# Score products of 128 rows with a copied low part of k, and a second gate projected ahead of the first branch product

## The chip, the cores and the metric

The kernel runs on one core of a Trainium2 chip. The metric is the device time of one execution in microseconds (us); the time of a kernel is the median over several executions. The core has five engines with a queue of instructions each: TensorE (PE in the profile; its weight loads are shown apart as PEld), VectorE (DVE), ScalarE (ACT), GpSimd (POOL) and SyncE (SP), which here issues nearly all of the transfers. On-chip memory is SBUF with 128 partitions; matmul results go to PSUM.

## The reference

One decoder layer on 1024 tokens of width 1024, in float32:

- `u = x * (1 + scale) + shift`, with shift, scale and gates from a small product of the conditioning vector.
- One projection of `u` gives q, k, v of two mixers and two gates of width 1024, `ga` and `gb`.
- Mixer a: 16 query heads of 64 over 2 key heads, causal window of 128, with a sink in the softmax denominator. Mixer b: 24 heads of 64 in three dilations (1, 4, 16), 8 heads each, whose outputs are weighted by the softmax of their log-sum-exps.
- Scores are `s = (q . k) / 8` in blocks of 128 queries against at most 256 keys.
- `merged = sigmoid(ga) * (oa @ w_branch_a) + sigmoid(gb) * (ob @ w_branch_b)`, then `merged @ w_o`, a residual with layer norm, a SwiGLU feed-forward of width 2816, and a second residual with layer norm.

## The kernel before, in words

**Exactness.** Matmuls take a rounded float32 format. An operand is therefore split into a high part (a rounding copy on ScalarE) and a low part (what is left, by a subtraction on VectorE), and a product is three matmuls: high x high, high x low, low x high (`mac`, lines 136 to 139, whose lines 137 to 139 lead the profile).

**Stage one, attention.** Twenty units follow each other: twelve of mixer b (four head pairs times three dilations, in the text "dilated units") and eight of mixer a ("window units"). A unit has two heads of 64 that lie in the lower and the upper 64 partitions. A generator `stream` yields the projections: of a dilated unit k, v and q, of a window unit q, and for the first of them also v and, last, k, which all eight share. One step of it is six matmuls; `pump` interleaves these steps with the four groups of scores of the unit before, the exponentials, the transposes of the probabilities (line 544) and the products with v (line 567). Work after a projection is put off by some steps (`soon`), so that TensorE doesn't wait for it. All of this is an order written by hand: each engine works its own queue in the order of the program.

The split of k is `k_stacks` (443 to 464). After rotary (GpSimd writes the result `r`, line 420), for each head ScalarE writes the high part `kh` twice, into the head's own 64 partitions (line 448) and into the other 64 (line 449), and VectorE writes the low part `kl` into the own half (line 454); only for the k that the window units share it writes the other half as well (line 456). The split of q (`q_stacks`) puts q's high part into the own half and its low part into the other. So one matmul of 128 rows against `kh` gives (high q + low q) x high k. A group of scores (`scores`, line 485) is for two blocks of queries and two heads: four such matmuls of 128 rows (line 495), then four of 64 rows with high q x low k (line 501), where the heads use different halves of the rows. A block is 256 keys wide, or 128 where there is no previous block.

**Weights.** `Weights` brings the weight pieces (256 KB each) in three raw buffers by SP (line 55), and splits them into four pairs of buffers `w_hi`, `w_lo` (lines 78 and 79). A piece is sent for as soon as a raw buffer is free; `step` splits the next one, at two points of a projection.

**Stage two, branch products.** For each of three branch halves (the two halves of `w_branch_a`, then `w_branch_b`) and eight column blocks `dc`, four split parts of the attention output, `o_hl` (line 117 high, 118 low), are multiplied with one weight piece and merged. Gates are projected in between by `make_gate` (48 matmuls, 16 groups of three): number 8 + dc for `ga`, 16 + dc for `gb`. Three gates (dc 3, 4, 5) are already projected in stage one, kept in device memory in `ga_d`, and only loaded. The list `order` fixes the sequence: gate 8 comes first, then products 0 to 7, then gate 9, product 8, gate 10, product 9 and so on. Ahead of gate 8 the parts of the first half are split (`o_parts`). Between gate groups and products `next(ada)` takes one of about forty small steps of a conditioning sum.

Of the kernel before, what the change touches and what calls it, by code (L numbers as in the profile page):

```python
# [10 lines left out]
F32 = mybir.dt.float32  # L11
F32R = mybir.dt.float32r
I32 = mybir.dt.int32
AF = mybir.ActivationFunctionType
OP = mybir.AluOpType
# [3 lines left out]
P = 128  # L19
T = 1024  # L20
# [78 lines left out]
def decoder_layer(ctx: ExitStack, tc: tile.TileContext, I, out, dbg=None):  # L99
    nc = tc.nc  # L100
# [54 lines left out]
    steps = [(b, dc) for b in range(3) for dc in range(KC)]  # L155
    gate_of = {8 + dc: 46 + dc for dc in range(KC)}
    gate_of.update({16 + dc: 54 + dc for dc in range(KC)})
    branch_w = [I["w_branch_a"][0], I["w_branch_a"][1], I["w_branch_b"]]
    made_early = [8 + dc for dc in (early_gate_dc, *tail_gates)]
    order = []  # L160
    for i in range(len(steps)):
        g = 8 if i == 0 else i + 1
        if g in gate_of and i != 7:
            order.append(("g", g))
        order.append(("w", i))
    for kind, i in order:
        if kind == "g" and i not in made_early:
            add_chunk(I["w_in"][gate_of[i]], 2, 4)
        elif kind == "w":
            b, dc = steps[i]  # L170
            add_chunk(branch_w[b][dc], 1, 4)
# [40 lines left out]
    ga_d = dram.tile([KC, P, T], F32, name="ga_d")  # L212
# [143 lines left out]
    att = ph1.enter_context(tc.tile_pool(name="att", bufs=2, side="right", reuse_waits="tile"))  # L356
# [69 lines left out]
    LO, HI = slice(0, 64), slice(64, 128)  # L426
# [13 lines left out]

        return rotary(e, r, then)

    def k_stacks(e, r, both, box):

        def stack(res, h):
            own, other = ((LO, HI), (HI, LO))[h]
            kh = att.tile([P, T], F32R, name="kh", bufs=4)
            nc.scalar.activation(kh[own], res[own], AF.Copy)
            nc.scalar.activation(kh[other], res[own], AF.Copy)
            box.setdefault("kh", []).append(kh)  # L450
            los = box.setdefault("kl", [])
            if both or not los:
                los.append(att.tile([P, T], F32R, name="kl", bufs=2))
            nc.vector.tensor_tensor(los[-1][own], res[own], kh[own], op=OP.subtract)  # L454
            if both:
                nc.vector.tensor_tensor(los[-1][other], res[own], kh[own], op=OP.subtract)
            elif h:
                los.append(los[0])

        def then(res):  # L460
            for h in range(2):
                soon(2 + h + (2 if e < EARLY else 0), lambda h=h: stack(res, h))

        return rotary(e, r, then)
# [20 lines left out]
    def scores(un, qr):  # L485

        box, prev, st = un["box"], un["prev"], un["st"]
        probs = att.tile([P, 2, 2, 2, P], F32, name="probs", bufs=2)
        un["probs", qr] = probs
        khs, kls = (box["kh"], box["kl"]) if "kv" not in un else ([kv_a["kh"][un["kv"]]] * 2, [kv_a["kl"][un["kv"]]] * 2)  # L490
        pss = [ps_s.tile([P, 2, 2, P], F32, name="s") for _ in range(2)]
        blocks = [(i, 2 * qr + i, 0 if prev(2 * qr + i) else 1) for i in range(2)]
        for i, b, lo in blocks:
            for h in range(2):
                nc.tensor.matmul(pss[h][:, i, lo:], box["q"][h][:, b * P:(b + 1) * P],  # L495
                                 khs[h][:, (b - 1 + lo) * P:(b + 1) * P], start=i == 0, stop=False,
                                 skip_group_check=True)

        for i, b, lo in blocks:
            for h, own in enumerate((LO, HI)):  # L500
                nc.tensor.matmul(pss[h][:, i, lo:], box["q"][h][own, b * P:(b + 1) * P],  # L501
                                 kls[h][own, (b - 1 + lo) * P:(b + 1) * P], start=False, stop=i == 1,
                                 skip_group_check=True)
        mx = att.tile([P, 2, 2], F32, name="mx", bufs=3)
        for h in range(2):
            for i, b, lo in blocks:
                nc.vector.tensor_tensor_reduce(  # L507
                    out=probs[:, h, i, lo:], in0=pss[h][:, i, lo:], in1=un["mask"][:, lo:], scale=QS, scalar=NEG,
                    op0=OP.add, op1=OP.max, accum_out=mx[:, h, i:i + 1])
            sl = slice(2 * qr, 2 * qr + 2)  # L510
            if "kv" in un:
                nc.vector.tensor_scalar(st[:, 0, h, sl], mx[:, h], un["sink"](h), -1.0, op0=OP.max, op1=OP.mult)  # L512
            else:
                nc.vector.tensor_scalar(st[:, 0, h, sl], mx[:, h], -1.0, None, op0=OP.mult)
# [150 lines left out]
    kv_a, units = {}, []  # L665
# [8 lines left out]
    def sigmoid_half(dst, ps):  # L674
        nc.scalar.activation(dst, ps, AF.Tanh, scale=0.5)
        nc.vector.tensor_scalar(dst, dst, 0.5, 0.5, op0=OP.mult, op1=OP.add)

    def stream():
        for un in units:
            if "b" in un:  # L680
                p, g = un["b"]
                base, r = (p * 3 + g) * 3, B_DIL[g]
                yield from k_stacks(base, r, False, un["box"])
                yield from values(base + 1, r, un["box"])
                yield from q_stacks(base + 2, r, un["box"])
            else:
                yield from q_stacks(36 + un["a"] + 2 * (un["a"] > 0), 1, un["box"])
                if un["a"] == 0:
                    yield from values(37, 1, kv_a)
                    yield from k_stacks(38, 1, True, kv_a)  # L690
        for dc in tail_gates:
            g = att.tile([P, T], F32, name="r", bufs=1)
            yield from project(46 + dc, lambda t, ps: sigmoid_half(g[:, t * TH:(t + 1) * TH], ps))
            nc.sync.dma_start(ga_d[dc], g)
# [49 lines left out]
    for s in range(len(subs) + 2):  # L744
        n, i = divmod(s, 4)
# [103 lines left out]
    ada = ada_steps()  # L849
    gts = {}  # L850

    def make_gate(i, *steps):
        g = mix.tile([P, T], F32, name="gt", bufs=2)
        gts[i] = g
        if i in made_early:
            nc.sync.dma_start(g, ga_d[i - 8])
            return
        ps = [ps_2.tile([P, TH], F32, name="p2") for _ in range(2)]
        for n, t in enumerate(gemm_u(ps, ws.take(2), *steps)):
            if n % 4 == 2:  # L860
                next(ada, None)
            if t is not None:
                sigmoid_half(g[:, t * TH:(t + 1) * TH], ps[t])

    def merge(b, dc, t, ps, g):
        m = mrg(dc, t)
# [18 lines left out]
                    nc.sync.dma_start(dbg["mg"][dc * P:(dc + 1) * P, t * TH:(t + 1) * TH], mrg(dc, t))  # L885

    for kind, i in order:
        if kind == "g":
            if i in (8, 9, 17):
                ws.prepare(4)  # L890
                parts = o_parts({8: 0, 9: 1, 17: 2}[i])
                make_gate(i, ())
            else:
                make_gate(i)
            if i == 23:
                mg = wide("m", bigu)
                split_merged(range(0, 3))
            continue
# [515 lines left out]
```

## Time and profile before

| | us |
|---|---|
| median of three runs | 1885.06 |
| lowest and highest run | 1883.31 and 1887.6 |
| the profiled execution's own time | 1886.68 |
| its span, first to last instruction | 1884.6 |
| TensorE busy in it | 1827.5 (97%) |
| VectorE, ScalarE, GpSimd busy | 1154.8, 784.0, 600.0 |

The mean granted clock of TensorE over the span is 0.992 of full speed. Busy time of an engine counts overlapping instructions once. A row of the profile has the line of the kernel, the engine, the operation, what is written <- what is read, shapes and a count; behind the bar stand total busy time and the mean in ns of one, and the engine's idle time in front with what ended it. A row of the order of time begins with the start in us from the span's start and the duration; a square bracket holds the idle time of the engine before it and what it waited for. `q` behind an engine is its queue of issues.

### The profile page before, as it was taken

Reading aid. Unit: us, or ns where it says so; the run is one execution under the profiler, and the core shown is the slowest. Engines: PE = TensorE matmul, PEld = TensorE weight load, DVE = VectorE, ACT = ScalarE, POOL = GpSimd, SP = SyncE. Lnnn points to the kernel's source line nnn. Section 1 sums busy time; section 2 is a strip of 40 time slices with the busy share of each in tenths; the row PEclk is TensorE's granted clock in tenths of the full one; section 3 lists DMA queues with packets and bytes.
Section 4 is the critical chain, followed back from the end, with each engine's and each line's share of the span. In section 5 each row is a group of like instructions: output and inputs, shape, how many; then the busy total and the mean of one; then the engine's idle time right before and its main releaser. Section 6 shows DMA issues by size and latency. Waiting matters only on the chain.

```text
span 1884.6 us, 24305 instructions
## 1 busy us (share of the span) xinstructions
PE 1827.5 (97%) x8924; PEld 1475.4 (78%) x8924; DVE 1154.8 (61%) x2136; ACT 784.0 (42%) x1664; POOL 600.0 (32%) x389
## 2 busy tenths in 40 slices
PE   6899999999999999989999999999999999999998
PEld 3678887877878767768888878878888888888886
DVE  5865567667667887643645365575565444674567
ACT  3544454544454667743112132653433333421122
POOL 2422323223223312100312242455664333531223
PEclk9999999999999999999999999999999999999999
DMA  8211112112111132144543223122222222442222
GB/s 280 91 34 35 35 36 79 40 39 76 42 57 63 41 95 76 57 168 155 208 137 137 79 72 134 57 90 101 85 78 85 89 79 89 151 134 71 97 84 89
DMA packets 72408, 171.85 MB, mean 91 GB/s; under 512 B 13089, under 2 KB 14177, under 8 KB 72290
## 3 DMA queue, kind: packets, MB, share of 16 engines
q1 hardware_dynamic: 71954, 169.26, 26.3%
q8 instruction: 70, 1.15, 0.3%
q0 software_dynamic: 336, 1.06, 0.2%
q14 instruction: 48, 0.39, 0.1%
HBM read 146.33 MB, written 23.95 MB: 90 GB/s over the span
## 4 chain that ended last, share of the span: by engine, by line
PE 81%; DVE 9%; ACT 4%; issue 3%; POOL 2%; DMA 1%; DVEq 0%; SPq 0%; POOLq 0%; ACTq 0%
PE pf L1108 22%; PE pj L137 7%; PE pj L139 7%; PE pj L138 6%; PE p L138 5%; PE p L139 5%; PE p L137 5%; PE pf L138 5%; PE pf L139 5%; PE pf L137 5%; PE pt L544 2%; PE po L567 2%; PE s L495 1%; PE s L501 1%; DVE probs L507 1%
## 5 line engine op out<-in xcount | busy, mean ns | idle before, releaser
L137 PE MATMUL pj<-u,w_hi 128*128 128x512 f32 x720 | 301.1, 418 | 0.0
L139 PE MATMUL pj<-u,w_lo 128*128 128x512 f32 x720 | 283.7, 394 | 0.0
L138 PE MATMUL pj<-u,w_hi 128*128 128x512 f32 x720 | 282.5, 392 | 0.0
L419 POOL TENSOR_TENSOR rb<-rb,sin_t 128x512 f32<-128x512 f32 x64 | 86.7, 1355 | 502.5 <-DVE rb L417 438.0
L118 DVE TENSOR_TENSOR w_lo<-r,w_hi 128x512 fp32r<-128x512 f32 x110 | 116.2, 1059 | 138.8 <-ACT w_hi L117 137.8
L79 DVE TENSOR_TENSOR w_lo<-w_raw,w_hi 128x512 fp32r<-128x512 f32 x148 | 131.2, 890 | 85.2 <-ACT w_hi L78 83.0
L522 ACT ACTIVATE probs<-probs,st 128x128 f32<-128x128 f32 (+1 forms) x320 | 146.0, 460 | 59.3 <-DVE st L512 30.1
L137 PEld LDWEIGHTS pj<-u,w_hi 128*128 128x128 f32 x720 | 136.2, 189 | 33.4 <-issue 4.7
L139 PEld LDWEIGHTS pj<-u,w_lo 128*128 128x128 f32 x720 | 135.8, 189 | 30.4
L138 PEld LDWEIGHTS pj<-u,w_hi 128*128 128x128 f32 x720 | 136.5, 190 | 22.4
L138 PE MATMUL pf<-wd,h 128*128 128x512 f32 x352 | 137.1, 389 | 0.0
L139 PE MATMUL pf<-wd,h 128*128 128x512 f32 x352 | 137.1, 389 | 0.0
L137 PE MATMUL pf<-wd,h 128*128 128x512 f32 x352 | 137.1, 389 | 0.0
L62 POOL TENSOR_TENSOR w_raw<-w_raw,gate 128x512 f32<-128x512 f32 x60 | 85.5, 1439 | 143.9 <-DMA w_raw<-in_w_down 120.6
L1327 DVE SCALAR_TENSOR_TENSOR zt<-zt,pf 128x512 f32<-128x512 f32 x112 | 75.3, 685 | 79.7 <-PE pf L139 79.7
L420 POOL TENSOR_TENSOR r<-ra,rb 128x512 f32<-128x512 f32 x63 | 114.5, 1817 | 6.1 <-DVE kl L454 1.3
L78 ACT ACTIVATE w_hi<-w_raw 128x512 fp32r<-128x512 f32 x148 | 90.8, 624 | 33.9 <-PE p L138 16.8
L546 ACT ACTIVATE ptsb<-pt 128x512 f32<-128x512 f32 (+1 forms) x128 | 63.5, 547 | 93.4 <-PE pt L544 93.0
L137 PE MATMUL p<-o_hl,w_hi 128*128 128x512 f32 x192 | 76.1, 396 | 6.8 <-ACT o_hl L117 6.8
L137 PE MATMUL p<-u,w_hi 128*128 128x512 f32 x208 | 82.2, 395 | 0.0
L139 PE MATMUL p<-u,w_lo 128*128 128x512 f32 x208 | 81.1, 390 | 0.0
L138 PE MATMUL p<-u,w_hi 128*128 128x512 f32 x208 | 81.0, 389 | 0.0
(305 smaller groups left out, 4266.8 us busy)
## 6 DMA issues: line engine op xcount, KB each, us to landing
w_raw<-in_w_in SPq DMA_DIRECT2D x116, 256.0 KB
r<-in_w_gate_up SPq DMA_DIRECT2D x47, 512.0 KB
a_raw<-in_w_ada SPq DMA_DIRECT2D x32, 512.0 KB
w_raw<-in_w_down SPq DMA_DIRECT2D x44, 256.0 KB
h_raw<-h_d SPq DMA_DIRECT2D x22, 512.0 KB
h_d<-g SPq DMA_DIRECT2D x40, 256.0 KB
wa<-in_w_ada_m SPq DMA_DIRECT2D x16, 512.0 KB
wb<-wt_d SPq DMA_DIRECT2D x24, 256.0 KB
```

What stands on the lines that cost most here:

```text
L62: self.nc.gpsimd.tensor_tensor(self.raws[i], self.raws[i], scale(), op=OP.mult)
L78: self.nc.scalar.activation(hi, raw, AF.Copy)
L79: self.nc.vector.tensor_tensor(lo, raw, hi, op=OP.subtract)
L118: nc.vector.tensor_tensor(lo, src, hi, op=OP.subtract)
L137: nc.tensor.matmul(ps, w[0], m[0], start=first, stop=False)
L138: nc.tensor.matmul(ps, w[0], m[1], start=False, stop=False)
L139: nc.tensor.matmul(ps, w[1], m[0], start=False, stop=last)
L419: eng.tensor_tensor(b, b, sin_t[:, s], op=OP.mult)
L420: eng.tensor_tensor(residue_half(res, r, t), by_residue(a, r), by_residue(b, r), op=OP.add)
L522: nc.scalar.activation(pr, pr, AF.Exp, bias=st[:, 0, h, b:b + 1], accum_out=st[:, 1, h, b:b + 1])
L1108: nc.tensor.matmul(ps, w[:, c], m[:, k], start=first and k == 0 and n == 0, stop=k == 3 and n == 2, skip_group_check=True)
L1327: nc.vector.scalar_tensor_tensor(z, z, ALPHA if gi == 0 else 1.0, pd, op0=OP.mult, op1=OP.add)
```

## The change

1. `k_stacks` makes both parts full height for every k: ScalarE writes `kh` into the own half only, VectorE `kl` into the own half only, and each is copied into the other half by a transfer that SP issues (SBUF to SBUF, 64 partitions x 4 KB). `kl` has four buffers in place of two.
2. `scores` uses `kl` with all 128 rows. For each block and head the product with `kh` is followed at once by that with `kl`; low q x low k is now part of the sum.
3. Gate 10 (dc 2 of `ga`) is projected right after gate 8, ahead of the first branch product, and written to `ga_d`. In its old place it is loaded, as the three early gates are. While it is projected no step of the conditioning sum is taken.

```diff
+    bridge = 10
     order = []
     for i in range(len(steps)):
         g = 8 if i == 0 else i + 1
         if g in gate_of and i != 7:
             order.append(("g", g))
+        if i == 0:
+            order.append(("b", bridge))
         order.append(("w", i))
     for kind, i in order:
-        if kind == "g" and i not in made_early:
+        if kind == "b" or (kind == "g" and i not in (*made_early, bridge)):
             add_chunk(I["w_in"][gate_of[i]], 2, 4)
...
-    def k_stacks(e, r, both, box):
+    def k_stacks(e, r, box):
...
             kh = att.tile([P, T], F32R, name="kh", bufs=4)
+            kl = att.tile([P, T], F32R, name="kl", bufs=4)
             nc.scalar.activation(kh[own], res[own], AF.Copy)
-            nc.scalar.activation(kh[other], res[own], AF.Copy)
+            nc.sync.dma_start(kh[other].bitcast(F32), kh[own].bitcast(F32))
+            nc.vector.tensor_tensor(kl[own], res[own], kh[own], op=OP.subtract)
+            nc.sync.dma_start(kl[other].bitcast(F32), kl[own].bitcast(F32))
             box.setdefault("kh", []).append(kh)
...
+            box.setdefault("kl", []).append(kl)
...
             for h in range(2):
-                nc.tensor.matmul(pss[h][:, i, lo:], box["q"][h][:, b * P:(b + 1) * P],
-                                 khs[h][:, (b - 1 + lo) * P:(b + 1) * P], start=i == 0, stop=False,
-                                 skip_group_check=True)
-
-        for i, b, lo in blocks:
-            for h, own in enumerate((LO, HI)):
-                nc.tensor.matmul(pss[h][:, i, lo:], box["q"][h][own, b * P:(b + 1) * P],
-                                 kls[h][own, (b - 1 + lo) * P:(b + 1) * P], start=False, stop=i == 1,
-                                 skip_group_check=True)
+                for n, ks in enumerate((khs, kls)):
+                    nc.tensor.matmul(pss[h][:, i, lo:], box["q"][h][:, b * P:(b + 1) * P],
+                                     ks[h][:, (b - 1 + lo) * P:(b + 1) * P], start=i == 0 and n == 0,
+                                     stop=i == 1 and n == 1, skip_group_check=True)
...
-    def make_gate(i, *steps):
+    def make_gate(i, *steps, kept=False):
         g = mix.tile([P, T], F32, name="gt", bufs=2)
         gts[i] = g
-        if i in made_early:
+        if i in (*made_early, bridge) and not kept:
             nc.sync.dma_start(g, ga_d[i - 8])
             return
         ps = [ps_2.tile([P, TH], F32, name="p2") for _ in range(2)]
         for n, t in enumerate(gemm_u(ps, ws.take(2), *steps)):
-            if n % 4 == 2:
+            if n % 4 == 2 and not kept:
                 next(ada, None)
             if t is not None:
                 sigmoid_half(g[:, t * TH:(t + 1) * TH], ps[t])
+        if kept:
+            nc.sync.dma_start(ga_d[i - 8], g)
...
     for kind, i in order:
+        if kind == "b":
+            make_gate(i, kept=True)
+            continue
```

How this moves the instructions, at the three places that the prediction speaks of. On ScalarE where k of the fourth unit is split while the third finishes, before:

```order
L448 ACTIVATE kh<-r 64x1024
L449 ACTIVATE kh<-r 64x1024
L78 ACTIVATE w_hi<-w_raw 128x512
L448 ACTIVATE kh<-r 64x1024
L449 ACTIVATE kh<-r 64x1024
L478 ACTIVATE vt<-pj 128x4x128
L78 ACTIVATE w_hi<-w_raw 128x512
L546 ACTIVATE ptsb<-pt 128x384 x2
```

and with the change (lines are numbered by the changed kernel):

```order
L452 ACTIVATE kh<-r 64x1024
L78 ACTIVATE w_hi<-w_raw 128x512
L452 ACTIVATE kh<-r 64x1024
L477 ACTIVATE vt<-pj 128x4x128
L78 ACTIVATE w_hi<-w_raw 128x512
L540 ACTIVATE ptsb<-pt 128x384 x2
```

Two copies (line 449) are gone ahead of the evacuation of v (`vt`) and of the transposed probabilities (`ptsb`).

On SP, where the k of the shared window unit is split, with the change (before there are six weight pieces in a row here):

```order
L55 DMA w_raw<-in_w_in 128x512 x4
L453 DMA kh<-kh 64x1024
L455 DMA kl<-kl 64x1024
L55 DMA w_raw<-in_w_in 128x512
L453 DMA kh<-kh 64x1024
L455 DMA kl<-kl 64x1024
L55 DMA w_raw<-in_w_in 128x512
L578 DMA st_d<-sr 32x128
```

Each head brings a copy of `kh`, which follows ScalarE, and one of `kl`, which follows VectorE, with a weight piece behind.

On ScalarE at the start of stage two (`o_hl`: the high part of the attention output; `gt`: a gate; `w_hi`: a weight piece; `zt`: the evacuated first product), before:

```order
L117 ACTIVATE o_hl<-o_raw 128x1024 x4
L675 ACTIVATE gt<-p_7735 128x512
L675 ACTIVATE gt<-p_7736 128x512
L78 ACTIVATE w_hi<-w_raw 128x512
L868 ACTIVATE zt<-p_7795 128x512
L868 ACTIVATE zt<-p_7796 128x512
```

and with the change:

```order
L117 ACTIVATE o_hl<-o_raw 128x1024 x4
L669 ACTIVATE gt<-p_7771 128x512
L669 ACTIVATE gt<-p_7772 128x512
L78 ACTIVATE w_hi<-w_raw 128x512
L669 ACTIVATE gt<-p_7832 128x512
L78 ACTIVATE w_hi<-w_raw 128x512
L669 ACTIVATE gt<-p_7833 128x512
L78 ACTIVATE w_hi<-w_raw 128x512
L864 ACTIVATE zt<-p_7899 128x512
```

Before, the first two products' weights are split ahead of these rows; with the change the four prepared pieces are the two gates', and the first product's piece is the first `w_hi` here, behind the four parts and gate 8.

More of the change, by code (lines that the diff above doesn't have):

```diff
@@ L447, in stack @@
             kh = att.tile([P, T], F32R, name="kh", bufs=4)
+            kl = att.tile([P, T], F32R, name="kl", bufs=4)
             nc.scalar.activation(kh[own], res[own], AF.Copy)
-            nc.scalar.activation(kh[other], res[own], AF.Copy)
+            nc.sync.dma_start(kh[other].bitcast(F32), kh[own].bitcast(F32))
+            nc.vector.tensor_tensor(kl[own], res[own], kh[own], op=OP.subtract)
+            nc.sync.dma_start(kl[other].bitcast(F32), kl[own].bitcast(F32))
             box.setdefault("kh", []).append(kh)
[L451 to L458, printed above, removed]
+            box.setdefault("kl", []).append(kl)
         def then(res):
@@ L682, in stream @@
                 base, r = (p * 3 + g) * 3, B_DIL[g]
-                yield from k_stacks(base, r, False, un["box"])
+                yield from k_stacks(base, r, un["box"])
                 yield from values(base + 1, r, un["box"])
@@ L689, in stream @@
                     yield from values(37, 1, kv_a)
-                    yield from k_stacks(38, 1, True, kv_a)
+                    yield from k_stacks(38, 1, kv_a)
         for dc in tail_gates:
```

## The prediction

> **What bounds the kernel now.** I read the page's busy times and the chain of waits first, then the groups of the lines that the diff touches, then the order of time around them.
>
> ```profile
> PE 1827.5 (97%) x8924; PEld 1475.4 (78%) x8924; DVE 1154.8 (61%) x2136; ACT 784.0 (42%) x1664; POOL 600.0 (32%) x389
> PE 81%; DVE 9%; ACT 4%; issue 3%; POOL 2%; DMA 1%; DVEq 0%; SPq 0%; POOLq 0%; ACTq 0%
> ```
>
> TensorE is the bound: the chain that ends last is 81% its own work. So an edit is worth what it takes out of TensorE's row of starts, or out of the waits in that row. Two stretches show whether other engines would take the time back (from and to, length, then the busy time and count of PE, PEld, DVE, ACT and POOL, granted clock, DMA share, GB/s):
>
> ```profile
> 100.00:240.00 140.00, 140.00 (x750) 112.94 (x750) 80.57 (x198) 71.57 (x173) 39.12 (x25) 0.99 0.10 35
> 627.00:697.00 70.00, 65.59 (x411) 49.32 (x409) 60.84 (x172) 48.67 (x141) 16.06 (x13) 1.00 0.24 73
> ```
>
> While the dilated units run (first row) no engine beside TensorE and its weight loads is busy more than 81 of 140 us. At the start of the window units (627 to 697) VectorE is busy for 61 of 70 us, so time saved on TensorE there may only lengthen a wait for it.
>
> **The scores.** The change replaces 320 matmuls of 64 rows by 320 of 128 rows:
>
> ```profile
> L495 PE MATMUL s<-kh,qs 128*128 128x256 f32 (+1 forms) x320 | 54.3, 285 | 9.4 <-DVE qs L434 5.8 <-DVE mx L507 3.6
> L501 PE MATMUL s<-kl,qs 64*128 64x256 f32 (+1 forms) x320 | 39.4, 325 | 0.0
> ```
>
> By busy time the small ones look cheaper (39.4 against 54.3 us), and the change a loss of 15 us. But busy time counts overlapping matmuls once, and what matters is when the next one starts. One group of eight, 256 wide, in order of time (start, duration):
>
> ```profile
> 105.42 0.63 PE L495 MATMUL s<-kh,qs 128*128 128x256 f32 x4
> 105.77 0.28 PE L495 MATMUL s<-kh,qs 128*128 128x256 f32 x1
> 105.98 0.50 PE L501 MATMUL s<-kl,qs 64*128 64x256 f32 x4
> 106.20 0.28 PE L501 MATMUL s<-kl,qs 64*128 64x256 f32 x2
> 106.41 0.50 PE L137 MATMUL pj<-u,w_hi 128*128 128x512 f32 x1
> 106.75 0.39 PE L138 MATMUL pj<-u,w_hi 128*128 128x512 f32 x1
> 106.98 0.40 PE L139 MATMUL pj<-u,w_lo 128*128 128x512 f32 x1
> ```
>
> A second row of the same kind starts later in the same four. The 128-row matmuls start every 0.117 us (105.42 to 105.77 in three steps). From the last of them to the first of 64 rows it takes 0.21. The four of 64 rows start in pairs, 0.22 apart: a pair takes as long as two of 128 rows one after the other (0.234), so the overlap saves almost nothing. The way back to 128 rows is paid again: 106.41 to 106.75 is 0.34, the step after it 0.23. With eight of 128 rows this group would last 8 x 0.117 + 0.23 = 1.17 us instead of 106.75 - 105.42 = 1.33: 0.16 saved. A group of 128-wide blocks and one of a window unit:
>
> ```profile
> 183.44 0.56 PE L495 MATMUL s<-kh,qs 128*128 128x128 f32 x4
> 183.50 0.50 PE L495 MATMUL s<-kh,qs 128*128 128x128 f32 x3
> 183.72 0.28 PE L495 MATMUL s<-kh,qs 128*128 128x128 f32 x1
> 184.63 0.40 PE L138 MATMUL pj<-u,w_hi 128*128 128x512 f32 x1
> 688.49 0.63 PE L495 MATMUL s<-kh,qs 128*128 128x256 f32 x4
> 689.49 1.09 PE L544 MATMUL pt<-ident,probs 128*128 128x128 f32 x8
> ```
>
> The 128-wide group: 0.06 + 7 x 0.11 + 0.23 = 1.06 against 184.63 - 183.44 = 1.19, so 0.13 saved. In the window units transposes follow the scores: 1.00 against 8 x 0.117 = 0.94, so 0.06 saved. Of the 80 groups (320 / 4) 16 are all 128 wide, 28 are followed by transposes, 36 are like the first: 36 x 0.16 + 16 x 0.13 + 28 x 0.06 = **9.5 us**. Bounds: 7.8 if the window units give nothing (busy VectorE), 12.8 if every group saves 0.16.
>
> [...]
>
> **The copies of k.** ScalarE loses 26 copies into the other half, VectorE two subtractions, and SP gains 52 transfers of 256 KB (kh and kl, two heads, 13 units). ScalarE's loss matters at one place per head pair, where k of the next pair is split:
>
> ```profile
> 285.27 1.06 ACT L449 ACTIVATE kh<-r 64x1024 fp32r<-64x1024 f32 x1
> ...
> 290.19 0.85 ACT L546 ACTIVATE ptsb<-pt 128x384 f32<-128x384 f32 x2
> 290.71 0.29 PE L581 MATMUL pt<-ident,st 128*32 128x128 f32 x1 [0.88 <-ACT ptsb L546]
> 293.31 0.55 PE L474 MATMUL pt<-ident,vt 128*128 128x128 f32 x3 [0.93 <-ACT vt L478]
> PEld pt L581 <- ACT ptsb L546: 3.4, 3, 1.1
> PEld pt L474 <- ACT vt L478: 4.1, 3, 1.4
> ```
>
> From the first of these rows to the last of ScalarE none has an idle time in front, and TensorE then waits for ScalarE twice, 0.88 and 0.93 us; the last two rows (total, times, longest) show it three times each. Two L449 of 1.06 stand in front, one for each head, so ScalarE is 2.1 us earlier and both waits go: 3 x 1.81 = **5.4 us**. Next due there is VectorE, which splits the same k behind ScalarE; I take 5.0, bounds 0 and 5.4.
>
> What the copies cost: SP works in order, so a copy that waits for ScalarE or VectorE holds the weight pieces and weight broadcasts behind it.
>
> ```profile
> 333.39 3.88 SPq L55 DMA_DIRECT2D w_raw<-in_w_in  x2
> 345.88 0.62 ACT L78 ACTIVATE w_hi<-w_raw 128x512 fp32r<-128x512 f32 x1
> 815.82 1.22 SPq L609 DMA_DIRECT2D wb<-wa_d  x2
> 820.63 1.23 DVE L618 TENSOR_TENSOR o<-o,wb 128x1024 f32<-128x1024 f32 x1 [5.28 <-DMA wb<-wa_d]
> 621.32 1.06 ACT L448 ACTIVATE kh<-r 64x1024 fp32r<-64x1024 f32 x1 [6.93 <-POOL r L420]
> 622.41 1.22 DVE L454 TENSOR_TENSOR kl<-r,kh 64x1024 fp32r<-64x1024 f32 x1 [1.10 <-ACT kh L448]
> 625.63 1.22 DVE L454 TENSOR_TENSOR kl<-r,kh 64x1024 fp32r<-64x1024 f32 x1
> 627.93 0.62 PE L495 MATMUL s<-kh,qs 128*128 128x128 f32 x4
> ```
>
> The first two rows are the shortest lead of a weight piece before the window units, 12.5 us from issue to use. No transfer from SBUF to SBUF is in the trace; the nearest are the two broadcasts of 256 KB, landed 4.8 us after the first issue. A copy pair holds SP from 622.4 (kh done) to 626.9 (second kl done), 4.5 us; 4.5 + 4.8 is under 12.5, so weights stay ahead. In dilated units v and q are projected after k, 16 steps of six matmuls, 1.4 us each at the pace of 0.23, which covers the landing. In the first window unit k comes last: kl is done at 623.6, lands by 628.4, and is wanted at 627.9. I take 0.7 us for this and the first unit of all, bounds 0 and 3.
>
> **The gate.** At the end of attention TensorE runs gate 8, then half of the first branch product, and stops:
>
> ```profile
> 836.46 0.39 PE L139 MATMUL p<-o_hl,w_lo 128*128 128x512 f32 x1
> 843.65 0.80 PE L137 MATMUL p<-o_hl,w_hi 128*128 128x512 f32 x1 [6.80 <-ACT o_hl L117]
> 842.54 2.00 ACT L117 ACTIVATE o_hl<-o_raw 128x1024 fp32r<-128x1024 f32 x2 [10.31 <-DMA oa_d<-o]
> 844.45 1.06 ACT L675 ACTIVATE gt<-p 128x512 f32<-128x512 f32 x2
> 847.24 0.68 DVE L79 TENSOR_TENSOR w_lo<-w_raw,w_hi 128x512 fp32r<-128x512 f32 x1
> 843.00:850.00 7.00, 5.89 (x13) 0.50 0.15 41
> 850.00:857.00 7.00, 7.00 (x32) 1.00 0.55 184
> ```
>
> (The last two rows are of TensorE alone: busy, count, granted clock, DMA share, GB/s.) The split of the third part waits until the last unit's output is stored. After the idle time the granted clock is 0.50, and 13 matmuls start where 32 do in the next 7 us: 19 x 0.219 = 4.2 us lost, and 6.3 before that (836.46 + 0.23 to 843.00), together 10.5. The product's first twelve matmuls end at 836.7, so they began 12 x 0.227 earlier, at 834.0; the moved gate puts 48 (10.9 us) in front, and TensorE reaches the product at 844.9. Late next are the product's own weights: they are now split behind the fourth part and gate 8 on ScalarE (842.54 + 1.06 + 1.06 + 0.63 = 845.3) and behind those on VectorE (about 847.1, near the 847.24 at which that queue reached its weight piece before). That leaves waits of 0.4 and 1.35: **8.5 us** gained, as 10.5 less 1.75, rounded down. Bounds: 10.5, and 5 if the clock falls again. At its old place the 48 matmuls go and five products follow each other instead of four; the gate comes back by a 512 KB load with a whole product of 5.5 us to spare, and costs nothing.
>
> [...]
>
> **Sum.** 9.5 + 5.0 + 8.5 - 0.7 = 22.3 us off the profiled execution's 1886.68 (span 1884.6 and 2.1 around it): 1864.4. That execution is 1.6 us above the median of the runs, 1885.06, so a median of about 1862.8; I say **1862**.
>
> **The rivals.** *The scores give nothing*: the time saved turns into waits for VectorE, which already leads in 627 to 697. For it: that row. Against it: 80.57 of 140 us in the dilated units, which hold 48 of the 80 groups. Without 9.5 us: 1872.
>
> *SP's queue ends the other way*: copies hold the weight pieces. It decides where hold plus landing exceed 12.5 us, that is with a hold of 7.7 us instead of 4.5; at 10.5 each of the 13 units loses 2.8 us, 36 us, less 22.3 gained: 1899, slower. Against it: the lead row, and that copies wait only for work that ends anyway.
>
> *The pairs were worth half*: if the gaps around the 64-row matmuls come with the change of operand and stay, and each group pays two more steps of 0.117, that is 80 x 0.234 = 18.7 us, less 8.5 + 5.0 - 0.7: 1891, slower. Against it: pairs 0.22 apart, and 106.75 to 106.98 changes operand without a gap. [...]
>
> *The boundary only moves*: the product waits for something else as long as before; 1886.68 - 9.5 - 5.0 + 0.7 - 1.6 = 1871.
>
> **How the numbers follow.** Forecast 0.70, its own range 1856 to 1869; no gain from the scores 0.11; boundary moves 0.09; SP's queue 0.05, half of it bad enough to end slower and the rest near no change; half-height pairs 0.03; 0.02 for a gain of nothing at all. The range of 1855 to 1875 takes in the bounds (12.8 + 5.4 + 10.5 would give 1856) and the two weaker gains. Faster by over 0.2% (3.8 us, about what a measurement here can tell) has the first three, 0.90; within it 0.045; slower 0.055.
>
> **What would show it.** Groups of scores that last about 1.17 us to the second projection matmul with no 0.21 or 0.34 step; no wait of L581 or L474 for ScalarE; in place of the 6.8 us idle one under 2 us for the weights, at granted clock 1.00; no new wait of TensorE for kh or kl beyond 1 us, and no wait for weight pieces. A forecast of this size is wrong if score matmuls wait for VectorE by what they save, or if a copy lands later than 5 us after its issue.

## The result, and the profile after

| | median, us | runs |
|---|---|---|
| before | 1884.32 | 1883.31 to 1887.60, 4 runs |
| after | 1872.64 | 1871.22 to 1874.15, 4 runs |

The ratio is 0.9935, 95% interval 0.9918 to 0.9952: faster by 11.7 us (9.0 to 15.5), about half of the 23 us that were forecast (1885.06 to 1862). The profiled execution after took 1871.44 us (span 1869.5), 15.2 less than the one before.

The chain of waits of the kernel after, by engine:

```profile
PE 75%; DVE 11%; ACT 4%; issue 4%; DMA 3%; POOL 2%; SPq 0%; DVEq 0%; ACTq 0%; POOLq 0%
```

TensorE's share of the chain fell from 81% to 75%; VectorE's rose from 9 to 11%, that of transfers from 1 to 3%. That points at new waits for VectorE and for transfers.

One group of score products after, in order of time on TensorE (start, duration), with the middle left out:

```profile
103.34 0.28 PE L495 MATMUL s<-kh,qs 128*128 128x256 f32 x1
103.46 0.28 PE L495 MATMUL s<-kl,qs 128*128 128x256 f32 x1
...
104.17 0.28 PE L495 MATMUL s<-kl,qs 128*128 128x256 f32 x1
104.29 0.40 PE L137 MATMUL pj<-u,w_hi 128*128 128x512 f32 x1
104.52 0.39 PE L138 MATMUL pj<-u,w_hi 128*128 128x512 f32 x1
```

The group lasts 104.52 - 103.34 = 1.18 us where 1.17 was predicted (1.33 before), without the steps of 0.21 and 0.34. So a group of this kind is as cheap as forecast, and most of the missing time is elsewhere. The place where a new head pair begins shows it. TensorE's waits there after:

```profile
287.92 0.65 PE L473 MATMUL pt<-ident,vt 128*128 128x128 f32 x4 [0.60 <-ACT vt L477]
294.87 0.55 PE L538 MATMUL pt<-ident,probs 128*128 128x128 f32 x3 [0.48 <-DVE v L474]
313.65 0.33 PE L495 MATMUL s<-kh,qs 128*128 128x128 f32 x1 [1.12 <-DVE qs L437]
```

and over the whole kernel (total, times, longest):

```profile
PE s L495 <- DVE qs L437: 3.3, 3, 1.1
PE pt L473 <- ACT vt L477: 1.8, 3, 0.6
PE pt L538 <- DVE v L474: 1.5, 3, 0.7
```

Before, TensorE waited at these places 3 x (0.88 + 0.93) = 5.4 us for ScalarE. After, it waits 1.8 for ScalarE and 3.3 + 1.5 for VectorE, 6.6 together. VectorE's own row after, at the same place:

```profile
291.78 1.23 DVE L648 TENSOR_TENSOR o<-o,wb 128x1024 f32<-128x1024 f32 x1 [4.81 <-DMA wb<-wt_d]
292.93 0.68 DVE L474 COPY v<-pt 128x512 f32<-128x512 f32 x1
...
299.41 3.08 DVE L648 TENSOR_TENSOR o<-o,wb 128x1024 f32<-128x1024 f32 x1
```

VectorE stands still 4.81 us for the first weight broadcast `wb` of the pair just finished, and everything in its queue (the copy of v, the rotation of q) stands behind. Before, the same wait was shorter and the broadcast landed sooner:

```profile
293.48 1.23 DVE L654 TENSOR_TENSOR o<-o,wb 128x1024 f32<-128x1024 f32 x1 [1.76 <-DMA wb<-wt_d]
305.03 1.21 DVE L654 TENSOR_TENSOR o<-o,wb 128x1024 f32<-128x1024 f32 x1
```

At the end of attention, the boundary, the rows after are one wait, and windows of TensorE alone (busy, count, granted clock, DMA share, GB/s):

```profile
839.52 0.50 PE L139 MATMUL p<-o_hl,w_lo 128*128 128x512 f32 x1 [0.81 <-DVE w_lo L79]
```

```profile
837.00:844.00 7.00, 6.19 (x28) 1.00 0.43 135
844.00:851.00 7.00, 7.00 (x33) 1.00 0.68 241
```

In place of the 6.80 us of idle time there is one wait of 0.81, and the clock stays at 1.00.

To place the time, the table gives for every kernel how much longer or shorter each stage of its profiled execution was than in the kernel before. Stage A runs from the first projection matmul (77.63 in the kernel before) to the one at 106.41, B (the dilated units) from there to the first projection matmul of the window units (617.87), C (the window units) to the first matmul of gate 8 (822.98), D (the boundary and the branches) to the first product of the merged branches (1112.83). What follows D moved by less than 1 us in each. The last column is the ratio of times with its interval.

| kernel | A | B | C | D | ratio to before |
|---|---|---|---|---|---|
| the change | -0.4 | -2.8 | -1.8 | -8.5 | 0.9935 [0.9918, 0.9952] |
| 1: gate 10 not moved | -1.8 | -2.8 | -1.7 | -1.5 | 0.9963 [0.9951, 0.9975] |
| 2: gate 10 alone | -1.2 | 0.0 | +0.4 | -6.3 | 0.9971 [0.9961, 0.9981] |
| 3: k written by engines | +2.1 | +5.5 | -0.8 | -6.3 | 0.9972 [0.9963, 0.9981] |
| 4: the change, broadcast earlier | -1.9 | -8.6 | -0.6 | -6.3 | 0.9899 [0.9886, 0.9911] |
| 5: before, broadcast earlier | -0.1 | +0.2 | +0.7 | +0.3 | 1.0004 [0.9995, 1.0013] |
| 6: copies on other queues | +0.7 | -1.9 | 0.0 | -7.8 | 0.9948 [0.9935, 0.9960] |
| 7: scores alone | -0.6 | -3.7 | -1.1 | +1.3 | 0.9975 [0.9966, 0.9985] |
| 8: ScalarE's relief alone | 0.0 | -4.7 | +0.5 | +0.9 | 0.9981 [0.9971, 0.9990] |
| 9: 4, and weights before the last part | -0.5 | -8.5 | -0.8 | -9.4 | 0.9892 [0.9876, 0.9907] |
| 10: 8, broadcast at its old place | +0.1 | -3.6 | +0.7 | -0.4 | 0.9980 [0.9971, 0.9988] |
| 11: 9, less for VectorE in C | -0.5 | -8.6 | -1.3 | -10.5 | 0.9886 [0.9868, 0.9904] |

The first projection matmul itself starts up to 1.7 us earlier or later from one execution to another (75.93 after, 77.63 before), ahead of anything that the change touches. So of the 15.2 us between the two profiles 1.7 are not the change's. And a row of the table is a single execution, which need not be a typical one: those of runs 3, 4 and 9 took 1886.94, 1869.52 and 1868.29 us, the longest of theirs, against medians of 1880.83, 1866.99 and 1865.44.

Four executions of 2000 to 3700 us (one of the kernel before beside runs 1 to 4, one each of runs 5, 11 and 12, that of run 12 the profiled one) are left out of the ratios; the medians below still hold them, and without them would be at most 0.6 us lower.

### The profile page after: what moved, and what is told of

Read it like the earlier page. It is cut to its first block, busy times and chain, and to the rows that moved or that the text cites. A ratio compares the mean times of both kernels' runs of the same rounds, so it can differ in the third digit from the quotient of the medians.

```text
span 1869.5 us, 24414 instructions
## 1 busy us (share of the span) xinstructions
PE 1815.1 (97%) x8924; PEld 1481.0 (79%) x8924; DVE 1157.7 (62%) x2134; ACT 758.4 (41%) x1638; POOL 602.1 (32%) x389
## 3 DMA queue, kind: packets, MB, share of 16 engines
q0 software_dynamic: 336, 1.06, 0.2%
## 4 chain that ended last, share of the span: by engine, by line
PE 75%; DVE 11%; ACT 4%; issue 4%; DMA 3%; POOL 2%; SPq 0%; DVEq 0%; ACTq 0%; POOLq 0%
PE pf L1107 21%; PE pj L137 6%; PE pj L139 6%; PE pj L138 6%; PE pf L138 5%; PE pf L137 5%; PE pf L139 5%; PE p L139 5%; PE p L138 5%; PE p L137 5%; PE s L495 2%; PE pt L538 2%; PE po L561 2%; DVE probs L501 1%; DMA wb<-wt_d 1%
## 5 line engine op out<-in xcount | busy, mean ns | idle before, releaser
L495 PE MATMUL s<-kh,qs 128*128 128x256 f32 (+1 forms) x320 | 80.9, 286 | 12.9 <-issue 5.5
```

## The experiments

The median of the kernel before was 1887.01 us beside runs 1 to 4, 1885.94 beside 5, 6, 7 and 9, 1885.70 beside 8, 10 and 11, 1885.77 beside 12.

**1 and 2: the two halves of the change.** Run 1 takes the moved gate out of the change, run 2 puts it alone into the kernel before:

```diff
-    if i == 0:
-        order.append(("b", bridge))
```

> The changed kernel with gate 10 back at its old place: scores and copies of k alone. Theory (the score groups gain about 9.6 us and the waits for ScalarE about 3, but in every head pair VectorE is held by a late first weight broadcast and gives most of it back): 4 to 6 us faster than before, about 1879, and the boundary shows its 6.8 us idle and half clock again. By the terms of the prediction (9.5 + 5.0 - 0.7): 13.8 us faster, about 1870.5. Rival (scores and copies give nothing, all of the gain is the boundary): 1884.

> The kernel before with gate 10 alone moved ahead of the first branch product: scores and k as before. Theory: 8.5 to 9.5 us faster, about 1875.5, and no slow clock behind the boundary. Rival (the boundary gave little by itself and the difference of the two traces there came from earlier stages): under 5 us faster, 1880 or more. With the run before this one the two should add up to the whole change, about 11.7 to 14 us; more or less by over 2 us says that the parts act on each other.

Measured: 1879.58 and 1880.45 us, 7.4 and 6.6 us faster. Scores and copies give half of their 13.8, a little more than the 4 to 6 of the theory; the gate gives 6.6 rather than 8.5 to 9.5. Together 14.0, against 11.7 (9.0 to 15.5) for the whole change: they add up within the intervals. What was expected of run 1's boundary missed in part: TensorE waits there 1.59, 1.00, 1.27 and 0.47 us in place of 6.80 and 0.46, and stage D gains 1.5, though the half clock comes as before (granted 0.60 from 830 to 837, 0.66 from 837 to 844). TensorE's row in run 2 shows why the gate alone gives less:

```profile
845.19 0.50 PE L137 MATMUL p<-o_hl,w_hi 128*128 128x512 f32 x1 [0.91 <-ACT w_hi L78]
845.53 0.39 PE L138 MATMUL p<-o_hl,w_hi 128*128 128x512 f32 x1
847.09 0.56 PE L139 MATMUL p<-o_hl,w_lo 128*128 128x512 f32 x1 [1.17 <-DVE w_lo L79]
847.44 0.63 PE L137 MATMUL p<-o_hl,w_hi 128*128 128x512 f32 x1
847.87 0.63 PE L138 MATMUL p<-o_hl,w_hi 128*128 128x512 f32 x1
```

These are the waits that the prediction had named (0.4 and 1.35, found 0.91 and 1.17), but behind them the matmuls start every 0.43 us instead of 0.23: the half clock is back (0.76 on average from 844 to 851), though TensorE never stood still for more than 1.17 us.

**3: the second halves of k written by the engines.** No transfers, and ScalarE and VectorE write both halves:

```diff
-            nc.sync.dma_start(kh[other].bitcast(F32), kh[own].bitcast(F32))
+            nc.scalar.activation(kh[other], res[own], AF.Copy)
-            nc.sync.dma_start(kl[other].bitcast(F32), kl[own].bitcast(F32))
+            nc.vector.tensor_tensor(kl[other], res[own], kh[own], op=OP.subtract)
```

> The changed kernel with the second halves of kh and kl written by ScalarE and VectorE from the rotated k in place of the 52 transfers: no copies on SP's queue, 26 copies more on ScalarE and 24 subtractions net more on VectorE than the kernel before has. Theory (transfers delay the first broadcast of each pair by about 1.2 us of hold and 1.2 us of slower landing): that broadcast lands as in the kernel before, 5.3 us after its issue, but VectorE has 2.4 us more work per pair in front of the scores, and the waits for ScalarE (0.88 and 0.93) are back: within 3 us of the changed kernel, 1870 to 1876. Rival (the transfers themselves are what is lost, by more than the engines' time): 3 to 6 us faster than the changed kernel, 1866 to 1869. Rival (VectorE is the bound in each pair): over 3 us slower than the changed kernel, 1876 or more.

Measured: 1880.83 us, 6.2 faster than before, all of it the gate's. (The expectation counts ScalarE's 26 second copies as more than the kernel before has; that kernel has them too.) TensorE's waits in run 3:

```profile
PE pt L473 <- ACT vt L477: 6.8, 5, 1.9
PE pt L575 <- ACT ptsb L540: 3.6, 3, 1.2
```

10.4 us for ScalarE in place of 5.4: with both halves written by engines the waits grow by 5.0, about what the scores give. Most of the +5.5 in stage B is the clock. At each head pair of this execution one of the waits is 1.9 us long, and the granted clock is halved behind it (TensorE alone, as above):

```profile
291.51:294.92 3.41, 1.52 (x10) 1.00 0.37 105
294.92:298.33 3.41, 3.41 (x14) 0.50 0.72 195
```

Three such stretches of 3.41 us at 0.50 are worth up to 5.1 us. They lie in the longest of the twelve executions of run 3, so by the times the scores' gain is lost and no more than that. So transfers are the better way to fill the second half, though they cost something; the rival that they are what is lost by more than the engines' time falls. VectorE is not the one waited for here, ScalarE is, so the third expectation holds in its number and not in its reason.

**4 and 5: the broadcast earlier.** The first weight broadcast of a pair is issued one score group sooner, ahead of the copies; in run 4 in the change, in run 5 in the kernel before:

```diff
             combine_weights(last["b"][0])
+            fetch_bcast((last["b"][0], 0), wt_d[last["b"][0], 0])
...
-            if i < 3:
+            if 0 < i < 3:
                 fetch_bcast((p, i), wt_d[p, i])
```

> The changed kernel with the first weight broadcast of a head pair issued one score group earlier, so ahead of the copies of k on SP's queue; its data and its reader stay. Theory (the late broadcast is what eats the gain): VectorE's wait of 4.8 us for it goes, TensorE's new waits of 0.5 and 1.1 us per pair shrink, 3 to 5 us faster than the changed kernel, about 1868. Rival (VectorE's own chain of combining and rotating is the bound there): the wait for the broadcast goes but the scores still wait for the second q, same time as the changed kernel within 1.5 us, about 1872.

> The kernel before with nothing changed but the first weight broadcast of a head pair issued one score group earlier, the same move as in the run before. It tells whether the copies of k made the broadcast a problem or whether it always was one. Theory (only the copies push it behind, and in the kernel before TensorE waits for ScalarE, not for VectorE): within 1.5 us of the kernel before, since VectorE's wait of 1.76 us for the broadcast is covered there. Rival (the late broadcast costs the kernel before as much, and the copies are innocent): 3 to 6 us faster than before.

Measured: run 4 1866.99 us, 20.0 faster than before, its interval clear of the change's; run 5 1887.47, no difference. VectorE and TensorE in run 4, where the change had waits of 4.81, 0.48 and 1.12:

```profile
287.14 1.20 DVE L648 TENSOR_TENSOR o<-o,wb 128x1024 f32<-128x1024 f32 x1
299.69 1.21 DVE L648 TENSOR_TENSOR o<-o,wb 128x1024 f32<-128x1024 f32 x1
```

```profile
PE pt L473 <- ACT vt L477: 1.9, 3, 0.7
```

VectorE no longer waits, its second multiplication takes 1.21 us instead of 3.08, and of the 6.6 us of waits at the head pairs 1.9 are left. Stage B goes from -2.8 to -8.6. In the kernel before the same move does nothing, so the late broadcast is a cost of the copies and not an old one.

**7 and 8: the prediction's two terms apart.** Run 7 is the kernel before with 128-row products that read kh twice (its expectation says what is left out); run 8 the kernel before with one edit in the split of k, and the broadcast moved as in run 5:

```diff
-            nc.scalar.activation(kh[other], res[own], AF.Copy)
+            nc.sync.dma_start(kh[other].bitcast(F32), kh[own].bitcast(F32))
```

> The kernel before with the 320 half-height score products replaced by 320 of 128 rows that read kh once more in place of kl (the low part of k is left out of the scores, so its time is that of the products alone): no transfers, k split as before, gate 10 at its old place. By the prediction's term: 9.5 us faster than before less what of it turns into waits for VectorE in the window units; 8 to 9.5. Rival (the time saved in the groups turns into waits for VectorE all along, and transfers have no part in it): 4 to 5 us, as the first run of the scores and copies gave within its noise. Rival (half-height pairs are worth their overlap): 0 or slower.

> The kernel before with only ScalarE's second copy of kh replaced by a transfer (26 transfers, half of the change's) and the first weight broadcast of a pair moved ahead of them: half-height scores, kl and gate 10 as before. It prices the prediction's second term without the others. Theory (the term was right, two L449 of 1.06 us out of ScalarE's row release TensorE twice per pair): the waits of 0.88 and 0.93 go or shrink to under 0.3, 4 to 5.4 us faster than before, ratio 0.997 to 0.998. Rival (TensorE would wait for VectorE at the same places): no gain, 1.000.

Measured: run 7 1881.10 us, 4.8 faster; run 8 1882.49 us, 3.2 faster. TensorE's waits in run 7 first, then its one wait at a pair in run 8:

```profile
PE s L496 <- DVE mx L502: 4.1, 10, 1.0
PE pt L576 <- ACT ptsb L541: 3.7, 3, 1.3
PE pt L474 <- ACT vt L478: 2.8, 3, 0.9
```

```profile
290.64 0.66 PE L474 MATMUL pt<-ident,vt 128*128 128x128 f32 x4 [0.26 <-ACT vt L478]
```

Run 7: with the scores alone the waits for ScalarE grow from 5.4 to 6.5 us, since TensorE arrives earlier at an engine that does not, and those for the score maxima (L507 in the kernel before, 3.6 us) to 4.1. Stage B gains 3.7. Run 8: the waits shrink from 1.81 to 0.26 a pair, stage B gains 4.7. The two add up to 8.4, and run 4, which has both, gains 8.6. But both runs give some back in D (+1.3, +0.9): with the gate at its old place TensorE stands at the boundary until the third part of the attention output is split, and ScalarE begins that 20.9 and 20.5 us after gate 8, against 19.6 in the kernel before. In run 10 it is 19.0, in run 1 14.4; why this moves was not traced.

**6 and 10: hold or landing.** Run 6 issues the copies of the change on other queues, run 10 is run 8 with the broadcast at its old place, behind two copies instead of four:

```diff
-            nc.sync.dma_start(kh[other].bitcast(F32), kh[own].bitcast(F32))
+            nc.scalar.dma_start(kh[other].bitcast(F32), kh[own].bitcast(F32))
-            nc.sync.dma_start(kl[other].bitcast(F32), kl[own].bitcast(F32))
+            nc.gpsimd.dma_start(kl[other].bitcast(F32), kl[own].bitcast(F32))
```

> The changed kernel with the copies of kh issued on ScalarE's queue and those of kl on GpSimd's, so that SP's queue holds no copy; the 52 transfers themselves stay. Theory in two halves: the broadcast was 1.2 us late by SP's queue being held and 1.2 us by a slower landing beside the copies. If the hold alone decides: ratio to before 0.990, as with the broadcast moved. If the sharing of the transfer engines decides: 0.9935, as the changed kernel. Half each: about 0.992. A loss (0.995 or more) would say that issuing from GpSimd holds the rotation behind it.

> The same as the run before it, with the broadcast at its old place behind the transfers. Theory (two transfers of 256 KB in flight beside the broadcast slow its landing about half as much as the change's four, which took it from 5.0 to 5.3 us to 6.5): the broadcast lands 5.7 to 6 us after its issue and about half of the gain is lost, ratio 0.998 to 0.9995. Rival (only four transfers or VectorE's own work make it late): the whole gain, as the run before it. Rival (any transfer there costs the whole gain): 1.000 or slower.

Measured: run 6 1875.87 us, not better than the change; run 10 1881.83 us, the same as run 8. SP's queue, with VectorE's wait behind it, in the change, in run 6 and in run 7 (which has no copies):

```profile
285.25 1.96 SPq L603 DMA_DIRECT2D wb<-wt_d  x2
```

```profile
285.37 1.45 SPq L603 DMA_DIRECT2D wb<-wt_d  x2
293.46 1.23 DVE L648 TENSOR_TENSOR o<-o,wb 128x1024 f32<-128x1024 f32 x1 [4.49 <-DMA wb<-wt_d]
301.09 3.09 DVE L648 TENSOR_TENSOR o<-o,wb 128x1024 f32<-128x1024 f32 x1
```

```profile
284.83 1.15 SPq L604 DMA_DIRECT2D wb<-wt_d  x2
289.86 1.22 DVE L649 TENSOR_TENSOR o<-o,wb 128x1024 f32<-128x1024 f32 x1 [1.45 <-DMA wb<-wt_d]
```

From issue to use the broadcast takes 5.0 us without copies, 6.5 in the change (285.25 to 291.78) and 8.1 in run 6, although no copy stands in SP's queue there. In the change SP's queue has a part too. Counted from the same projection matmul (283.70 in the kernel before, 279.57 in the change, 281.11 in run 6), the broadcast is issued after 4.4, 5.7 and 4.3 us and used after 9.8, 12.2 and 12.4: it is 2.4 us late in the change, half of that by its issue behind the copies and half by its landing. Run 6 takes the first half away, and the landing grows by as much, so it is the transfers in flight that decide. Run 6 has a cost of its own besides: TensorE waits 3.5 us for copies of kl there, three times, the longest 1.5. The windows of the traces before and after say the same (busy and count of PE, PEld, DVE, ACT and POOL, granted clock, DMA share, GB/s):

```profile
283.00:291.00 8.00, 7.12 (x47) 5.37 (x46) 4.73 (x14) 6.69 (x10) 1.15 (x1) 1.00 0.25 74
```

```profile
283.00:291.00 8.00, 7.40 (x52) 5.48 (x51) 3.84 (x14) 5.39 (x16) 0.00 (x0) 1.00 0.98 235
```

The transfer engines were a quarter busy in these 8 us (0.25), and are now full (0.98). In run 6, with the copies on other queues, they are busy by 0.84 from 283 to 293, and the broadcast takes its 8.1 us; in run 7, without copies, by 0.45 from 283 to 291, and it takes 5.0.

Run 10 shows what lateness must do before it costs anything. Its broadcasts landed 6.6, 5.6 and 5.8 us after their issue. VectorE in its first and in its second head pair, and TensorE's wait for q in the first:

```profile
302.64 3.10 DVE L654 TENSOR_TENSOR o<-o,wb 128x1024 f32<-128x1024 f32 x1
...
436.94 1.21 DVE L654 TENSOR_TENSOR o<-o,wb 128x1024 f32<-128x1024 f32 x1
```

```profile
316.90 0.55 PE L495 MATMUL s<-kh,qs 128*128 128x128 f32 x3 [0.79 <-DVE qs L434]
```

Only in the first pair did the second multiplication take 3.10 us, and only there did TensorE wait for q by more than 0.15 us. I had expected that half the lateness would cost half the gain. It cost a whole step in one pair of three and next to nothing in the others; in stage B it is 1.1 us, too little for the times to show.

**9, 11 and 12: better versions.** Run 9 is run 4 with the product's own weights split ahead of the fourth part on ScalarE and VectorE; run 11 gives, in addition, the last pair's three multiplications by the weights to GpSimd; run 12 is run 2 with run 9's edit:

```diff
-                parts = o_parts({8: 0, 9: 1, 17: 2}[i])
+                parts = o_parts(b, range(3 if b == 0 else 4))
                 make_gate(i, ())
+                if b == 0:
+                    ws.prepare(3)
+                    parts += o_parts(b, range(3, 4))
```

```diff
-        nc.vector.tensor_tensor(og, og, sums.pop((p, g)), op=OP.mult)
+        eng = nc.gpsimd if p == B_PAIRS - 1 else nc.vector
+        eng.tensor_tensor(og, og, sums.pop((p, g)), op=OP.mult)
```

> The changed kernel with the broadcast moved, and the first branch product's own weights split ahead of the fourth part of the attention output on ScalarE and VectorE. In the run with the broadcast moved alone, TensorE waited 0.69 and 0.97 us for those weights and ran 8 matmuls at 0.43 us in place of 0.23 behind them. Theory (two waits of under 1 us so close together are enough for the slow clock): both waits and the slow stretch go, 3.3 us faster than that run, ratio to before about 0.988. Rival (the fourth part is then what the product waits for, as long as before): no faster than that run, 0.990.

> The run with the product's weights split ahead of the last part, and the three multiplications of 128x1024 that combine the last dilated pair (1.2 us each on VectorE, about 650 to 670 us, in the window units) given to GpSimd. It asks why the score products gain nothing in the window units once TensorE is early there. Theory (VectorE's row of work is the bound at 650 to 690, where TensorE's waits for the score maxima sum to about 4 us): 1 to 2.5 us faster than that run, ratio 0.988 or lower. Rival (the bound is the chain of one group, scores to maxima to exponentials, and not VectorE's load): within 0.7 us of it, 0.989. Rival (GpSimd slows VectorE beside it): slower, 0.990 or more.

> The kernel before with gate 10 ahead of the first branch product and, added, that product's own weights split ahead of the fourth part: scores and k as before. With the gate alone TensorE waited 0.91 and 1.17 us, two matmuls apart, and the next nine matmuls ran at half clock, 1.8 us: 3.9 us in all, and the whole was 6.6 us faster than before. Theory (the two short waits and the half clock behind them are what was missing to the 10.5 us of the boundary): no wait and no half clock there, 9.5 to 10.5 us faster than before, ratio about 0.9947. Rival (the fourth part or a later wait takes the place): 0.9965 or more.

Measured: 1865.44, 1865.44 and 1879.00 us (run 12: 0.9963 [0.9949, 0.9977]). In run 9's profile the boundary has no wait and no slow clock; TensorE alone, as above:

```profile
833.00:840.00 7.00, 7.00 (x32) 1.00 0.39 98
840.00:847.00 7.00, 7.00 (x32) 1.00 0.87 311
```

and stage D gains 9.4 instead of 6.3. But its time is not clearly below run 4's, and run 12 is 6.8 us faster than before where run 2 was 6.6: the expected 3 us are not in the times. Run 12's profile cannot be set beside the others, so what takes the place there stays open. Run 11 is within 0.6 us of run 9 in stage C (-1.3 against -0.8), as its first rival had it. But run 9's execution has 3.41 us of half clock in that stage, from 668.57 on, worth up to 1.7 us, and run 11's has none. So less work for VectorE gained nothing there that these runs show; that the chain from scores to maxima is the bound is not shown. All of runs 4, 9 and 11 beat both kernels; their intervals do not tell them apart.

## Why the prediction was half right

**The scores, 9.5 us.** Right for a group of 256-wide blocks (1.18 us measured, 1.17 predicted), too high for other reasons. The first and the last score product of an all-128 group after, and the two projection matmuls behind it:

```profile
180.28 0.22 PE L495 MATMUL s<-kh,qs 128*128 128x128 f32 x1
...
181.01 0.28 PE L495 MATMUL s<-kl,qs 128*128 128x128 f32 x1
181.12 0.44 PE L137 MATMUL pj<-u,w_hi 128*128 128x512 f32 x1
181.40 0.39 PE L138 MATMUL pj<-u,w_hi 128*128 128x512 f32 x1
```

It lasts 1.12 and not 1.06, since the step back to the projection is 0.28 where 0.23 was assumed, and saves 0.07 instead of 0.13: 16 x 0.06 = 1.0 us too much. And the waits for ScalarE grow by 1.1 us when TensorE comes earlier (run 7); the term was worked out as if the time behind each group were free. Run 7 prices the term at 3.7 us in B and 1.1 in C, where the prediction had 7.8 for all dilated units and 1.7 for the window units. Of the groups counted as dilated, two lie in A and five in C; for about 1 us of the rest in B I found no row. In the times it is 4.8 us.

**ScalarE's waits, 5.0 us.** Right: run 8 gains 4.7 in stage B by this alone, and run 4 with run 7 gives 8.6 - 3.7 = 4.9. Not all of the waits went, as the prediction's sentence had it: the one for v is 0.26 us per pair in run 8, and 0.6 in the change and in run 4, where the scores bring TensorE there earlier.

**The copies, 0.7 us, bounds 0 and 3.** This step failed. It set SP's hold (4.5 us) and the landing of the copies themselves (4.8 us) against the lead of the weight pieces (12.5 us), and that part held: no row shows TensorE waiting for the landing of a weight piece, and with the copies on SP's queue its longest wait for a copied kl is 0.4 us (run 4). It also said that a held queue holds the weight broadcasts, but gave them no price. The broadcast `wb` has VectorE as its reader and no lead: it is issued 1.2 us later behind the copies, and lands 6.5 us after its issue instead of 5.3. The trace of before had that row with its idle time of 1.76 in front, and the prediction did not ask what stands behind it. The price is what run 4 takes back in stage B, 8.6 - 2.8 = 5.8 us, 1.9 per pair, beyond the bound of 3.

How 2.4 us of lateness become 1.9 us per pair: VectorE works in order, so the copy of v comes late (0.48 on TensorE), and then its second multiplication begins just after GpSimd has begun its half of the rotation:

```profile
299.02 2.38 POOL L423 TENSOR_TENSOR r<-ra,rb 128x512 f32<-128x512 f32 x1
```

From 299.41 it takes 3.08 us in place of 1.21; q is rotated late, and the scores wait 1.12. At the first pair this collision is in the change and in runs 6 and 10 (3.08, 3.09 and 3.10 us), and not in runs 4 and 7 (1.21 and 1.22 at most). GpSimd ends at 301.40 and the multiplication at 302.49, 1.09 us later; at the change's other two pairs and in runs 6 and 10 it is 1.08 to 1.10 us later too, a little less than the 1.21 that it takes alone. In runs 4 and 7 it is the split of a weight's low part that begins beside GpSimd's row there: it takes 1.93 us in place of 0.69, and ends 0.55 and 0.56 us after it. So in these rows VectorE's instruction ends as if it had begun only when GpSimd's was over; what makes it so is not shown. "Next due there is VectorE" stood in the prediction, with a lower bound of 0 for the term; the likeliest value should have been nearer to it.

**The gate, 8.5 us.** The changed kernel's profile has 8.5, with one wait of 0.81 instead of 0.4 and 1.35. In runs 2 and 4 both waits came and the clock fell with them (0.76 on average from 844 to 851, 0.80 from 837 to 844), and 6.3 was left: the bound "5 if the clock falls again" was the right one to keep. So that the change's profile meets the 8.5 is in part luck: by the times the gate alone gave 6.6. The 8.5 counts on a full clock behind waits of 0.4 and 1.35 us, which no run shows: run 4's two waits, two matmuls apart, are shorter together (1.66 against 1.75), and the matmuls behind them start every 0.43 us instead of 0.23.

**The rivals.** The measured 1872.6 is just the time of the rival in which the scores give nothing, but not its mechanism: run 7 has the scores give 4.8 us, and the loss is the copies'. It lies within the range of 1855 to 1875, which takes in two weaker rivals, and outside the forecast's own 1856 to 1869: the range held, and the sum did not. No row shows TensorE held up by a weight piece on SP's queue. The half-height pairs were not worth their overlap: run 7 is 4.8 us faster, not slower. The boundary did not only move: run 2 gains 6.6 us.

**Where the 22.3 us went**, profile against profile: predicted 12.8 in A and B with the copies' share (7.8 + 5.0), 1.7 in C, 8.5 in D, less 0.7. Found 3.3, 1.8 and 8.5, together 13.6, and 1.7 at the start which is not the change's.

## What to carry to other kernels

When a change swaps an engine's work for transfers, price not only the transfers' landing but that of every other transfer in flight beside them (here 5.3 us became 6.5), and look up who reads it: the one without a lead is what pays. Put a transfer that an in-order engine will wait for ahead of the bulk, as early as its data allow; here one transfer moved was worth 5.8 us in stage B. And measure the terms of a sum alone: the scores and ScalarE's relief added up to within 0.2 us once the thing between them was out of the way.

## What the runs showed of the hardware that I had not expected

*Two short waits, or one of 1.9 us, can halve the clock.* In run 2 waits of 0.91 and 1.17 us with two matmuls between them brought a row of matmuls at 0.43 us each; in run 4 waits of 0.69 and 0.97 did the same, and in run 3 one wait of 1.89; a single wait of 0.81 in the changed kernel did not. So 1.66 us of idle time in all were enough in run 4. From 100 us on, the granted clock in the profiles of the two kernels and of runs 1 to 11 changes only in steps of 3.41 us, which lie differently in each execution: in the kernel before it is 0.50 from 839.80 to 850.04, three steps. Every step behind which the clock fell had at least 1.64 us without a matmul; no step with 1.56 us or less was followed by a fall, and neither were five with 1.75 to 1.9. So the idle time in a step does not decide by itself whether the clock falls; what else does is not shown.

*The slow clock behind one idle gap lasts differently from run to run.* At the first scores of all TensorE idles 5.0 us in the kernel before. In it and in run 2, which are alike there, the clock came back at different times (TensorE alone, as above), before and then run 2:

```profile
100.00:104.00 4.00, 4.00 (x13) 0.69 0.00 0
```

```profile
100.00:104.00 4.00, 4.00 (x19) 1.00 0.00 0
```

Six matmuls more in the same 4 us: this is about the -1.2 of stage A in run 2, in which nothing was changed. Differences of a microsecond between two single profiles have to be looked for here first.
